# The first norm's modulation vectors in plain fp32 through four column groups of TensorE, and a new order of the first 190 steps

## The chip, the cores and the metric

One core of one Trainium2 chip runs the whole block. The metric is the device time of one launch in microseconds (us), median of several runs. The engines are named as in the profile: PE is TensorE's matmuls, PEld its weight loads, DVE VectorE, ACT ScalarE, POOL GpSimd, SP the engine whose queue issues nearly all loads.

## The reference

One layer of a diffusion block over 1024 latent tokens with 256 context tokens, width 1024, all in fp32:

```python
sh1, sc1, g1, sh2, sc2, g2 = adaln(c, w_mod, b_mod)        # silu(c) @ w_mod + b_mod, in six pieces
csh1, csc1, ... = adaln(c_ctx, w_mod, b_mod)
hc = modulate(ctx, norm1_w, csh1, csc1)                     # rmsnorm(x) * w * (1 + scale) + shift
state = context_state(hc, w_in, b_in)
h = modulate(x, norm1_w, sh1, sc1)
out, _ = token_mixers(h, w_in, b_in, ..., state, grid=True)
x = x + g1 * out
x = x + g2 * ffn(modulate(x, norm2_w, sh2, sc2), w_ff1, w_ff2)
return rmsnorm(x, final_norm_w)
```

The change concerns sh1, sc1, csh1, csc1 alone: two vectors (c and c_ctx) times the first 2048 columns of w_mod, 8 MB of weights.

## The kernel before

A large product is made from two fp32r halves of each operand, hi (the rounded value) and lo (the rest): three matmuls (hi hi, hi lo, lo hi) take the place of one in fp32. ACT rounds hi, DVE or POOL subtracts for lo.

The first stage ends with the keys, queries and first values of heads 0 and 1. It is written out by hand in ORDER: a list of steps, each a letter and a number, and every engine's instructions keep this order. Each engine's queue runs in order, so an instruction that waits holds up all behind it on its engine. The steps:

- mN loads piece N (128 x 1024, 512 KB) of the modulation weights; 2k and 2k+1 are the two halves of the contraction for feature block k (128 features; shift and scale for them).
- oN makes the lo half of piece N where it has one, on DVE or POOL (LO_G).
- rk is the matmuls of feature block k: the stationary operand is silu of the two vectors, the moving one the weights, the result a PSUM bank "o". yk copies it to SBUF (mrow). ck turns it with the small matrix comb from rows into columns (PSUM tile psu), and DVE adds the bias and forms 1 + scale (mod1).
- xN, hN, nN load a tile of 128 tokens, square and sum it on ACT, and scale it on DVE to xh. Tiles 0 to 3 are the first half of the tokens, 4 to 7 the second, 8 and 9 the context.
- fgk, ugk, jgk take feature block k of token group g (g is left out for 0): f transposes four tiles on PE, u applies the modulation and rounds to hh, j subtracts for hl. For odd k, u runs on ACT and j on POOL, else DVE.
- w, z load and split the weights of keys (w0) and queries (w1); gk is the six matmuls of 512 columns that add feature block k to keys and queries. v, b load and split the value weights (v0s), t and s make the values of a chunk of 128 tokens. e takes keys and queries out of PSUM.

Keys and queries of a token half need all eight feature blocks, so g7 waits for the last modulation piece. PSUM banks "o" exist twice, "g" three times, others once. After the list, the rest of the kernel follows: recurrence, gates, output projections and the MLP. Its code is not touched. SP's loads are issued in order, and each waits for the landing of the load eight places before it.

Before, ten of the sixteen pieces are split into hi and lo (whi, wlo, with the vectors split too, silr), six (F32N) are used in fp32 with the vectors in sil4:

```python
for j in range(4):
    for i, (a, w_) in enumerate(ops):
        PE.matmul(b, a[:, 4 * (n % 2) + j, :], w_[:, j * 256 : j * 256 + 256], ...)
```

All four j add into the same four rows of the bank, b[0:4].

Of the kernel before, what the change touches and what calls it, by code (L numbers as in the profile page):

```python
# [22 lines left out]
NPG = 37  # L23
NPG2 = 4
PUMP = 1300.0
F32N = (1, 2, 3, 4, 5, 8)
LO_G = (1, 4, 5, 6, 9, 11, 12, 15)

ORDER = (
# [6 lines left out]
)  # L36
MOD_RATE = 0.16
YC = 448
# [11 lines left out]
CST = {}  # L50
_off = 0
for _name, _n in (("ident", 128), ("mask", 256), ("ones", 128), ("ident2", 128), ("flip", 128), ("dsel", 128), ("t2", 64), ("tri", 256), ("e", 8), ("sel", 16), ("selt", 128), ("selc", 16), ("selct", 32), ("ec", 2), ("comb", 2)):
    if _name == "ident2":
        NCST0 = _off
# [6 lines left out]
def tile_block(ctx: ExitStack, tc: tile.TileContext, x, cx, w_mod1, w_mod, w_v0, w_v, w_unit, w_conv, w_mls, w_o, w_f1, w_f2, cols_d, rows_d, cst_d, out):  # L61
# [20 lines left out]
    V, A, G, PE, SY = Engine(nc.vector), Engine(nc.scalar), Engine(nc.gpsimd), Engine(nc.tensor), nc.sync  # L82

    cpool = ctx.enter_context(tc.tile_pool(name="cpool", bufs=1))
    dpool = ctx.enter_context(tc.tile_pool(name="dpool", bufs=1, space=bass.MemoryType.DRAM))
    pg = ctx.enter_context(tc.tile_pool(name="pg", bufs=NPG))
    ws = ctx.enter_context(tc.tile_pool(name="ws", bufs=2))
# [5 lines left out]
    def dma(dst, src, pin=True):  # L93
        i = SY.dma_start(dst, src)
        if pin:
            tc.keep_in_program_order(i)
# [3 lines left out]
    def nm(s):  # L100
        uid[0] += 1
        return f"{s}_{uid[0]}"

    def page(shape, dt=F32, name="pg"):
        return pg.tile(shape, dt, tag="pg", name=nm(name))

    def half(name):
        return ws.tile([P, 512], F32, tag="half", name=nm(name), bufs=4)

    cols = cpool.tile([P, NCOL], F32, name="cols")  # L110
    cst0 = cpool.tile([P, NCST0], F32, name="cst0")
# [84 lines left out]
    def bank(tag="g"):  # L196
        if tag == "g":
            pool = psg
            if psg2:
                pool = (psg, psg2[0])[turn[0] % 8 > 2]  # L200
                turn[0] += 1
            return pool.tile([P, 512], F32, tag="g", name=nm("psg"))
        return psm.tile([P, 512], F32, tag=tag, name=nm("ps" + tag), bufs=2 if tag == "o" else 1)
# [3 lines left out]
    A.activation(sig, col("c2", 0, 16), AF.Sigmoid)  # L207
    sil = cpool.tile([P, 8, 2], F32, name="sil")
    V.tensor_tensor(sil, col("c2", 0, 16).rearrange("p (v k) -> p k v", v=2), sig.rearrange("p (v k) -> p k v", v=2), op=ALU.mult)
    silr = cpool.tile([P, 8, 4], F32R, name="silr")  # L210
    V.tensor_copy(silr[:, :, 0:2], sil)
    V.tensor_tensor(silr[:, :, 2:4], sil, silr[:, :, 0:2].bitcast(F32), op=ALU.subtract)
    sil4 = cpool.tile([P, 8, 4], F32, name="sil4")
    V.memset(sil4, 0.0)
    V.tensor_copy(sil4[:, :, 0:2], sil)

    eps_c = cpool.tile([P, 1], F32, name="eps_c")
    V.memset(eps_c, EPS)
# [16 lines left out]
        dma(st, src)  # L235
        return wide(st, **kw)

    dma(cst0, cst_d[:, :NCST0])

    def rstd_of(xt, scratch):  # L240
        ss = ws.tile([P, 1], F32, tag="ss", name=nm("ss"))
        keep(A.activation)(scratch, xt, AF.Square, accum_out=ss)
# [10 lines left out]
        return b[:, : len(tiles) * P]  # L253


    comb = ws.tile([4, 2], F32, tag="comb", name="comb", bufs=1)
    dma(comb, cst_d[0:4, CST["comb"][0] : CST["comb"][0] + 2])
    mcol = bank("u")
    loads, lows = {}, {}
    mod1 = cpool.tile([P, 2, 2, 8], F32, name="mod1")  # L260
# [2 lines left out]
    def mod_load(n):  # L263
        w = page([P, 1024], name="wmod")
        dma(w, w_mod1[n // 2, n % 2])
        if n in F32N:
            return [(sil4, w)]
        hi, lo = [page([P, 1024], F32R, t_) if n % 2 else ws.tile([P, 1024], F32R, tag=t_, name=nm(t_)) for t_ in ("whi", "wlo")]
        A.activation(hi, w, AF.Copy)
        lows["o", n] = lambda: (G if n in LO_G else V).tensor_tensor(lo, w, hi.bitcast(F32), op=ALU.subtract)  # L270
        return [(silr, hi), (silr, lo)]

    def mod_rows(k):

        b = bank("o")[0:4, 0:256]
        for n in (2 * k, 2 * k + 1):
            ops = loads.pop(n)
            for j in range(4):
                for i, (a, w_) in enumerate(ops):
                    PE.matmul(b, a[:, 4 * (n % 2) + j, :], w_[:, j * 256 : j * 256 + 256], start=n % 2 == 0 and j == 0 and i == 0, stop=n % 2 == 1 and j == 3 and i == len(ops) - 1)  # L280
        return b

    def mod_cols(k, r):
# [67 lines left out]


    gb = wm.tile([P, 32], F32, name="gb", bufs=1)
    dma(gb, rows_d[0:1, 1024:1056].to_broadcast([P, 32]))

    gz = wm.tile([P, 2, 160], F32, tag="e", name="gz", bufs=3)

    def v_out(p):
        vb = wm.tile([P, 256], F32, tag="vb", name=nm("vb"), bufs=1)
        dma(vb, rows_d[0:1, p * 256 : p * 256 + 256].to_broadcast([P, 256]), pin=p == 0)  # L360
        va = [page([P, 2, 4, 129], name="va") for _ in range(2)]
        vc = wm.tile([P, 2, 2, 129], F32, tag="vc", name=nm("vc"), bufs=1)
        for t_ in (*va, vc):
            G.memset(t_[:, :, :, 128:129], 1.0)
        return va, vc, vb
# [332 lines left out]
    vs0 = (*v_out(0), wv0, 288)  # L698
# [28 lines left out]
    def item(i):  # L727

        op, n = i[0], int(i[1:])
        g, k = divmod(n, 10)
        if op == "m":
            loads[n] = mod_load(n)
        elif op in "obz":
            lows.pop((op, n), int)()
        elif op == "r":
            made[op, n] = mod_rows(n)  # L740
        elif op == "y":
            r = half("mrow")[0:4, 0:256]
            V.tensor_copy(r, made.pop(("r", n)))
            made[op, n] = r
        elif op == "c":
            mod_cols(n, made.pop(("y", n)))
        elif op == "x":
            load(n)
        elif op == "h":
            square(n)  # L750
        elif op == "n":
            hat(n)
        elif op == "f":
            if n == 20:
                for h_ in (hch, hcl):
                    h_ += [page([P, 1024], F32R, "hc") for _ in range(2)]
            made[op, n] = transposed(TILES[g], k)
        elif op == "u":
            hi, _, sh, sc = feat(g, k)
            made[op, n] = modulate(made.pop(("f", n)), hi, sh, sc, k)  # L760
        elif op == "j":
            hi, lo, _, _ = feat(g, k)
            (G if k % 2 else V).tensor_tensor(lo, made.pop(("u", n)), hi.bitcast(F32), op=ALU.subtract)
        elif op == "w":
            st = ws.tile([P, 1024], F32, tag="wst", name=nm("wst"))
            dma(st, w_unit[(U_K, U_Q)[n]])
            hi, lo = page([P, 1024], F32R, "whi"), page([P, 1024], F32R, "wlo")
            A.activation(hi, st, AF.Copy)
            lows["z", n] = lambda: V.tensor_tensor(lo, st, hi.bitcast(F32), op=ALU.subtract)
            wkq.append((hi, lo))  # L770
        elif op == "g":
            if k == 0:
                accs[g] = [bank(), bank()]
            gemm_k(wkq, hT, g, accs[g], k)
        elif op == "e":
            evac_k(0, kT0, accs[n][0], n)
# [238 lines left out]
    m2 = cpool.tile([P, 4, 8], F32, name="m2")  # L1015
# [262 lines left out]
    t2 = [None] * KT  # L1278
# [230 lines left out]
    b12, b22, t1, t4, t2_ = (lambda k: feat2(f1, k)), (lambda k: feat2(f1, 4 + k)), (lambda k: feat2(f0, k)), (lambda k: feat2(f0, 4 + k)), (lambda k: feat2(t2f, k))  # L1509
# [177 lines left out]
    for i in range(tail):  # L1687
        m, k = steps[i]
# [3 lines left out]
        o = Y if m in (5, 6, 3) else X  # L1692
# [9 lines left out]
        if i == 3:  # L1702
            g2 = grow(3, Y[0:2])
# [9 lines left out]
        if k == NP - 1:  # L1713
# [17 lines left out]
            elif m == 3:  # L1731
                a, b, c, d = [gated_sum(j, R, Y[j], ub[j]) for j in (2, 3, 0, 1)]
# [8 lines left out]
    for j in range(4):  # L1741
        t = 4 + j
        cuts = (0, 512) if j < 3 else (0, CUT, 512)
        n = len(cuts)
# [5 lines left out]
        for c in range(1, n):  # L1750
            s = slice(cuts[c - 1], cuts[c])
            w = cuts[c] - cuts[c - 1]
# [24 lines left out]
def _layout(i):  # L1777
# [11 lines left out]
    o = {}  # L1789
# [6 lines left out]
    v0 = np.concatenate([wv[:, 0:256], w_in[:, 1536:1568]], axis=1)  # L1796
# [19 lines left out]
    r = np.arange(P)  # L1816
# [10 lines left out]
    sel = (d_ * 8 + h_)[:, None] == dh[None, :]  # L1827
    selc = ((rc // 16) * 8 + rc % 8)[:, None] == dh[None, :]
    comb = np.zeros((P, 2))
    comb[[0, 2], 0] = 1  # L1830
    comb[[1, 3], 1] = 1
    cst = {
        "ident": eye, "ident2": eye, "flip": eye[::-1], "dsel": (d_[:, None] == d_[None, :]) * 1.0,
        "t2": (r[:, None] % 64 == np.arange(64)[None, :]) * 1.0,
# [28 lines left out]
```

## Time and profile before

| | |
|---|---|
| median of 3 runs | 1784.93 us (1784.78 to 1785.35) |
| profiled execution | 1784.66 us |
| its span | 1782.9 us |
| PE busy | 1738.9 us (98%) |
| DVE, ACT, POOL busy | 1269.6, 754.8, 192.8 us |
| mean DMA rate | 146 GB/s; 325 in the first fortieth of the span |
| PE, first work | at 11.21 us |

The span is the stretch from the first to the last instruction; the profiled execution's time has 1.8 us around it. Times below are counted from the span's start. An idle time in a row stands in brackets with what ended it. A matmul in fp32 shows as two records (it runs in two passes), one in fp32r as one. Records of a matmul overlap with the next, so work is read from start to start.

### The profile page before, as it was taken

The page shows a single profiled execution, that of the slowest core. Times are in us where ns is not written, and L with a number is a line of the kernel's source. Part 1 is how long each engine was busy: PE and PEld are TensorE (multiplying, and loading weights), DVE is VectorE, ACT ScalarE, POOL GpSimd, SP SyncE. Part 2 cuts the span into 40 slices and gives each one's busy share as a digit, 9 for nine tenths or more (in the row PEclk, how much of TensorE's full clock was granted, in tenths as well). Part 3 has the DMA queues.
Part 4 walks back from the last instruction along what each step waited for, and adds up shares of the span by engine and source line. Part 5 has one row for each costly group of instructions (what it writes and reads, how often), then busy time and mean ns, then how long its engine had stood idle before and what let it go on. Part 6 is the DMA issues. An engine that isn't in the chain of part 4 may idle for free.

```text
span 1782.9 us, 23518 instructions
## 1 busy us (share of the span) xinstructions
PE 1738.9 (98%) x8633; PEld 1433.6 (80%) x8633; DVE 1269.6 (71%) x2224; ACT 754.8 (42%) x1239; POOL 192.8 (11%) x269
## 2 busy tenths in 40 slices
PE   7999999999999999999999999999999999999994
PEld 3898889877878888888888888877888888888884
DVE  5557565564876669878889987877666656577785
ACT  5633544556343332222244435644444354343434
POOL 3202122212300000000000001111011000000001
PEclk9999999999999999999999999999999999999997
DMA  8213131321534452433647255135334285665352
GB/s 325 77 47 91 46 93 43 89 70 61 174 145 142 157 197 97 140 131 124 228 167 284 71 207 183 72 138 187 130 141 178 112 279 194 233 230 199 104 181 94
DMA packets 102108, 261.11 MB, mean 146 GB/s; under 512 B 11624, under 2 KB 24808, under 8 KB 101992
## 3 DMA queue, kind: packets, MB, share of 16 engines
q1 hardware_dynamic: 85672, 200.88, 34.5%
q0 software_dynamic: 16320, 58.73, 8.3%
q8 instruction: 67, 1.10, 0.3%
q14 instruction: 49, 0.40, 0.1%
HBM read 198.62 MB, written 60.95 MB: 146 GB/s over the span
## 4 chain that ended last, share of the span: by engine, by line
PE 65%; DVE 4%; ACT 2%; issue 1%; ACTq 0%; DVEq 0%
PE psg L75 65%; ACT y L75 1%; DVE wlo L75 1%; DVE gate L75 0%; DVE wst L75 0%; ACT Fsh L75 0%; DVE y L75 0%; ACT fc L75 0%; DVE fc L75 0%; DVE Gv L75 0%; DVE x L75 0%; DVE ftmp L75 0%; DVE Ff L75 0%; DVE Fsl L75 0%; DVE u L75 0%
## 5 line engine op out<-in xcount | busy, mean ns | idle before, releaser
L75 DVE TENSOR_TENSOR wlo<-wst,whi 128x512 fp32r<-128x512 f32 (+1 forms) x236 | 223.5, 950 | 144.5 <-ACT whi L75 144.0
L75 ACT ACTIVATE whi<-wst 128x512 fp32r<-128x512 f32 (+1 forms) x238 | 195.8, 826 | 262.4 <-PE psg L75 170.4
L75 PE MATMUL psg<-whi,wlo 128*128 128x512 f32 (+2 forms) x688 | 266.2, 387 | 0.0
L75 PE MATMUL psg<-whi 128*128 128x512 f32 (+2 forms) x688 | 266.2, 387 | 0.0
L75 PE MATMUL psg<-wlo,whi 128*128 128x512 f32 (+2 forms) x688 | 265.7, 386 | 0.1
L75 PE MATMUL psg<-hh,whi 128*128 128x512 f32 x440 | 176.0, 406 | 0.0
L75 PE MATMUL psg<-hh,wlo 128*128 128x512 f32 x440 | 172.7, 398 | 1.3 <-DVE wlo L75 1.3
L75 PE MATMUL psg<-hl,whi 128*128 128x512 f32 x440 | 172.0, 397 | 0.0
L75 PEld LDWEIGHTS psg<-wlo,whi 128*128 128x128 f32 x688 | 129.3, 188 | 28.0 <-DVE wlo L75 0.6
L75 PEld LDWEIGHTS psg<-whi,wlo 128*128 128x128 f32 x688 | 129.2, 188 | 27.3
L75 PEld LDWEIGHTS psg<-whi 128*128 128x128 f32 x688 | 129.2, 188 | 27.0
L75 PEld LDWEIGHTS psg<-hh,wlo 128*128 128x128 f32 x440 | 83.1, 189 | 20.5 <-DVE wlo L75 1.7
L75 PEld LDWEIGHTS psg<-hl,whi 128*128 128x128 f32 x440 | 83.1, 189 | 17.3
L75 PEld LDWEIGHTS psg<-hh,whi 128*128 128x128 f32 x440 | 82.4, 189 | 17.9
L75 PE MATMUL psg<-oh,Fsl 128*128 128x512 f32 x240 | 94.8, 395 | 0.1
L75 PE MATMUL psg<-oh,Fsh 128*128 128x512 f32 x240 | 94.9, 395 | 0.0
L75 PE MATMUL psg<-ol,Fsh 128*128 128x512 f32 x240 | 94.5, 394 | 0.0
L75 DVE TENSOR_TENSOR u<-psg,u 128x512 f32<-128x512 f32 x67 | 45.8, 686 | 51.5 <-PE psg L75 51.5
L75 PE MATMUL psg<-whi,hh 128*128 128x256 f32 (+1 forms) x256 | 76.0, 297 | 0.0
L75 PE MATMUL psg<-wlo,hh 128*128 128x256 f32 (+1 forms) x256 | 73.2, 286 | 0.0
L75 PE MATMUL psg<-whi,hl 128*128 128x256 f32 (+1 forms) x256 | 73.1, 286 | 0.0
L75 POOL TENSOR_TENSOR wqz<-w,q 64x256 f32<-64x256 f32 x64 | 48.9, 768 | 159.1 <-PE pso L75 141.2
(347 smaller groups left out, 3868.3 us busy)
## 6 DMA issues: line engine op xcount, KB each, us to landing
wst<-fq SPq DMA_DIRECT2D x112, 256.0 KB, 2.8
wst<-in_w_unit_dram SPq DMA_DIRECT2D x38, 512.0 KB, 5.2
mst<-in_w_mod_dram SPq DMA_DIRECT2D x32, 512.0 KB, 4.3
fq<-Ff POOLq DMA_DIRECT2D x32, 512.0 KB, 4.2
wst<-in_w_f_dram SPq DMA_DIRECT2D x64, 256.0 KB, 3.1
wst<-in_w_f_dram SPq DMA_DIRECT2D x21, 512.0 KB, 4.3
Hwst<-in_w_unit_dram SPq DMA_DIRECT2D x18, 512.0 KB, 5.2
x<-in_x_dram SPq DMA_DIRECT2D x16, 512.0 KB, 6.0
```

The source lines that it names most:

```text
L75: i = f(*a, **kw)
```

## The change

All sixteen pieces are used in fp32. The vectors stand in sil32, whose rows 2 to 31 are zero, so that a matmul fills 32 columns of the array; the four j of a piece go to four groups of 32 columns and to four groups of 32 rows of the bank (rows 32j and 32j+1 hold the result). comb, now 128 rows, adds the four groups up in ck. The splits of the modulation weights and steps o are gone. The loads of comb and of the first constants (cst0, with the identity for transposes) move from the front into a step k0, those of the biases gb and vb into a step l0. The list is in a new order up to where the second half begins, and beyond it.

```diff
-    silr = cpool.tile([P, 8, 4], F32R, name="silr")
...
-    V.tensor_copy(sil4[:, :, 0:2], sil)
+    sil32 = page([P, 8, 32], name="sil32")
+    G.memset(sil32, 0.0)
+    V.tensor_copy(sil32[:, :, 0:2], sil)
...
-    dma(cst0, cst_d[:, :NCST0])
...
-        if n in F32N:
-            return [(sil4, w)]
-        hi, lo = [page([P, 1024], F32R, t_) if n % 2 else ws.tile([P, 1024], F32R, tag=t_, name=nm(t_)) for t_ in ("whi", "wlo")]
-        A.activation(hi, w, AF.Copy)
-        lows["o", n] = lambda: (G if n in LO_G else V).tensor_tensor(lo, w, hi.bitcast(F32), op=ALU.subtract)
-        return [(silr, hi), (silr, lo)]
+        return w
...
-        b = bank("o")[0:4, 0:256]
+        b = bank("o")[:, 0:256]
         for n in (2 * k, 2 * k + 1):
-            ops = loads.pop(n)
+            w = loads.pop(n)
             for j in range(4):
-                for i, (a, w_) in enumerate(ops):
-                    PE.matmul(b, a[:, 4 * (n % 2) + j, :], w_[:, j * 256 : j * 256 + 256], ...)
+                PE.matmul(b[32 * j : 32 * j + 32, :], sil32[:, 4 * (n % 2) + j, :], w[:, j * 256 : j * 256 + 256], start=n % 2 == 0, stop=n % 2 == 1, skip_group_check=True)
...
-            r = half("mrow")[0:4, 0:256]
+            r = half("mrow")[:, 0:256]
...
+        elif op == "k":
+            dma(comb, cst_d[:, CST["comb"][0] : CST["comb"][0] + 2])
+            dma(cst0, cst_d[:, :NCST0])
+        elif op == "l":
+            dma(gb, rows_d[0:1, 1024:1056].to_broadcast([P, 32]))
+            dma(vs0[2], rows_d[0:1, 0:256].to_broadcast([P, 256]))
...
-    "x0 m0 x2 h0 m1 x3 o1 h3 o0 x1 n3 m2 m3 m4 h2 n2 o3 h1 r0 n1 o4 o2 y0 n0 r1 y1 c0 m6 f0 m5 m7 m9 o5 o6 f1 u0 r2 m8 y2 c1 "
+    "m3 x2 x1 x3 h3 x0 h2 h0 n2 h1 m2 m0 r1 n3 m1 n0 r0 y1 k0 n1 m7 f0 y0 f1 m4 c0 c1 f2 m5 u0 m6 r2 r3 y2 m8 j0 c2 u1 m9 "
...
```

What it does to the order, on PE at the very start. Before, the last pair of r0's first piece (split) and its second piece (in fp32, with sil4, here sil), then r1, c and the transposes of f0:

```order
L75 MATMUL pso_187<-whi_143,silr 4x256
L75 MATMUL pso_187<-wlo_144,silr 4x256
L75 MATMUL pso_187<-wmod_153,sil_86 4x256 x4
L75 MATMUL pso_208<-wmod_168,sil_86 4x256 x4
L75 MATMUL pso_208<-wmod_170,sil_86 4x256 x4
L75 MATMUL psu_95<-comb,mrow_203 128x2 x2
L75 MATMUL psm_60_228<-cst_67,xh_148 128x128
```

Now r1, r0, and then the transposes of f0:

```order
L73 MATMUL pso_169<-wmod_165,sil_2_83 32x256 x4
L73 MATMUL pso_169<-wmod_132,sil_2_83 32x256 x4
L73 MATMUL pso_186<-wmod_167,sil_2_83 32x256 x4
L73 MATMUL pso_186<-wmod_181,sil_2_83 32x256 x4
L73 MATMUL psm_55_204<-cst_67,xh_152 128x128
```

Each r is eight matmuls of 32 rows by 256 columns where it was eight to sixteen of 4 rows by 256; the first transposes come before the first use of comb.

On SP, the first loads before (x the tokens, wmod the pieces m):

```order
L94 DMA cols<-in_cols_dram 128x168
L94 DMA cst_67<-in_cst_dram 128x512
L94 DMA comb<-in_cst_dram 4x2
L94 DMA gb<-in_rows_dram 128x32
L94 DMA vb_131<-in_rows_dram 128x256
L94 DMA x_139<-in_x_dram 128x1024
L94 DMA wmod_141<-in_w_mod_dram 128x1024
L94 DMA x_146<-in_x_dram 128x1024
```

And now, from the start:

```order
L92 DMA cols<-in_cols_dram 128x168
L92 DMA wmod_132<-in_w_mod_dram 128x1024
L92 DMA x_134<-in_x_dram 128x1024
L92 DMA x_136<-in_x_dram 128x1024
L92 DMA x_138<-in_x_dram 128x1024
L92 DMA x_145<-in_x_dram 128x1024
L92 DMA wmod_165<-in_w_mod_dram 128x1024
L92 DMA wmod_167<-in_w_mod_dram 128x1024
L92 DMA wmod_181<-in_w_mod_dram 128x1024
L92 DMA comb<-in_cst_dram 128x2
L92 DMA cst_67<-in_cst_dram 128x512
```

Four small loads left the front; the four token tiles and the first pieces moved up. gb and vb now stand behind the weights of keys and queries (w0, w1), and m15 behind the first value weights.

On PE where the products g begin (hh, hl are the modulated tokens; whi and wlo the split weights of keys and queries where they stand with them, of a piece m where they stand with silr). Before, the end of r5's 16 matmuls, behind g0 and g1, and then g2:

```order
L75 MATMUL pso_413<-whi_346,silr 4x256
L75 MATMUL pso_413<-wlo_347,silr 4x256
L75 MATMUL psg_379<-hh_99,whi_282 128x512
L75 MATMUL psg_380<-hh_99,whi_333 128x512
L75 MATMUL psg_379<-hl_107,whi_282 128x512
L75 MATMUL psg_380<-hl_107,whi_333 128x512
```

Now, the end of g0, then c4, r5 and g1:

```order
L73 MATMUL psg_333<-hh_92,wlo_273 128x512
L73 MATMUL psg_334<-hh_92,wlo_299 128x512
L73 MATMUL psu_90<-comb,mrow_308 128x2 x2
L73 MATMUL pso_353<-wmod_311,sil_2_83 32x256 x4
L73 MATMUL pso_353<-wmod_306,sil_2_83 32x256 x4
L73 MATMUL psg_333<-hh_93,whi_272 128x512
L73 MATMUL psg_334<-hh_93,whi_298 128x512
```

Before, g2 was followed by r6 and r7, and g3 to g7 came behind them; now it is g0, c4, r5, g1, c5, r6, g2, c6, r7, f7, g3, c7, and g4 to g7. Behind g7 the instructions on PE are the same as before, in another order: t1, then three transposes of the second token half, t2, and so on.

## Rows read from the trace of the kernel before

**Rows 1.** Windows, whole core: length, busy (instructions) of PE, PEld, DVE, ACT, POOL; PEclk, DMA share.

```profile
11.20:59.02 47.82, 45.28 (x241) 28.00 (x241) 35.41 (x55) 30.88 (x48) 20.71 (x9) 0.96 0.71 270
59.02:107.29 48.27, 48.27 (x338) 45.95 (x336) 19.12 (x51) 24.93 (x45) 8.16 (x10) 1.00 0.13 47
107.29:1760.00 1652.71, 1645.10 (x8059) 1359.61 (x8057) 1203.58 (x2087) 684.73 (x1118) 158.45 (x237) 1.00 0.43 145
```

**Rows 2.** Groups by form, PE, 11.2 to 59.02.

```profile
L75 PE MATMUL pso<-wmod,sil 128*4 128x256 f32 x48 | 12.9, 430 | 0.0
L75 PE MATMUL pso<-whi,silr 128*4 128x256 f32 x40 | 10.4, 294 | 11.2 <-ACT whi L75 11.2
```

**Rows 3.** Timeline, PE, 11 to 36: start, us, engine, operation, count.

```profile
14.06 7.38 PE L75 MATMUL pso<-wmod,sil 128*4 128x256 f32 x24
21.36 0.60 PE L75 MATMUL psu<-comb,mrow 4*128 4x2 f32 x4
...
22.92 3.62 PE L75 MATMUL pso<-wmod,sil 128*4 128x256 f32 x16
...
33.95 0.60 PE L75 MATMUL psm<-cst,xh 128*128 128x128 f32 x4
34.39 0.60 PE L75 MATMUL pso<-cst,xh 128*128 128x128 f32 x4
```

**Rows 4.** Windows at the changes of the granted clock.

```profile
18.20:38.70 20.50, 19.23 (x117) 11.48 (x116) 15.21 (x26) 13.37 (x16) 9.78 (x5) 1.00 0.90 360
38.70:42.10 3.40, 3.40 (x9) 2.18 (x10) 3.40 (x3) 0.30 (x1) 3.40 (x2) 0.50 0.70 221
```

**Rows 5.** Timeline, PE, 39 to 59.

```profile
39.11 1.05 PE L75 MATMUL psg<-hh,whi 128*128 128x512 f32 x2
39.97 1.05 PE L75 MATMUL psg<-hl,whi 128*128 128x512 f32 x2
...
57.64 0.63 PE L75 MATMUL psg<-hh,whi 128*128 128x512 f32 x2
58.11 0.62 PE L75 MATMUL psg<-hl,whi 128*128 128x512 f32 x2
```

**Rows 6.** Timeline, PE, the instant 219.9, and what follows.

```profile
219.68 0.28 PE L75 MATMUL psg<-whi,hl 128*128 128x256 f32 x1
219.88 0.38 PE L75 MATMUL psm<-q,kT 64*128 64x128 f32 x2
...
220.31 0.39 PE L75 MATMUL psg<-whi,hh 128*128 128x256 f32 x1
```

**Rows 7.** Timeline, ACT, 10 to 29.

```profile
10.10 1.06 ACT L75 ACTIVATE whi<-wmod 128x1024 fp32r<-128x1024 f32 x1 [5.74 <-DMA wmod<-in_w_mod_dram]
...
13.96 1.06 ACT L75 ACTIVATE xh<-x 128x1024 f32<-128x1024 f32 x1 [1.44 <-DMA x<-in_x_dram]
...
24.14 1.06 ACT L75 ACTIVATE whi<-wmod 128x1024 fp32r<-128x1024 f32 x1 [0.22 <-DMA wmod<-in_w_mod_dram]
...
27.75 0.78 ACT L75 ACTIVATE mtmp<-pso,mod 128x512 f32<-128x512 f32 x1 [2.03 <-PE psm L75]
28.56 0.63 ACT L75 ACTIVATE hh<-mtmp 128x512 fp32r<-128x512 f32 x1
```

**Rows 8.** Groups by form, ACT, 11 to 59.02.

```profile
L75 ACT ACTIVATE whi<-wmod 128x1024 fp32r<-128x1024 f32 x10 | 10.3, 1049 | 9.6 <-DMA wmod<-in_w_mod_dram 9.6
```

**Rows 9.** Groups by form, DVE, 11 to 59.02.

```profile
L75 DVE TENSOR_TENSOR wlo<-wmod,whi 128x1024 fp32r<-128x1024 f32 x5 | 7.6, 1515 | 7.7 <-ACT whi L75 7.7
...
L75 DVE COPY mrow<-pso 4x256 f32<-4x256 f32 x8 | 3.3, 409 | 4.6 <-PE pso L75 4.6
```

**Rows 10.** Groups by form, POOL, 11 to 59.02.

```profile
L75 POOL TENSOR_TENSOR wlo<-wmod,whi 128x1024 fp32r<-128x1024 f32 x5 | 14.0, 2813 | 25.4 <-ACT whi L75 25.4
L75 POOL TENSOR_TENSOR hl<-mtmp,hh 128x512 fp32r<-128x512 f32 x4 | 6.8, 1697 | 9.5 <-ACT hh L75 9.5
```

**Rows 11.** DMA rate over 0 to 40, in 40 slices of 1 us.

```profile
GB/s 0 52 157 169 82 210 329 401 418 414 426 410 422 426 397 410 418 414 397 430 422 397 426 410 406 401 414 418 406 401 422 410 410 397 414 324 89 41 24 59
```

More of the change, by code (lines that the diff above doesn't have):

```diff
@@ L25 @@
 PUMP = 1300.0
-F32N = (1, 2, 3, 4, 5, 8)
-LO_G = (1, 4, 5, 6, 9, 11, 12, 15)
 ORDER = (
[6 rows of a table removed]
[6 rows of a table added]
 )
@@ L209, in tile_block @@
     V.tensor_tensor(sil, col("c2", 0, 16).rearrange("p (v k) -> p k v", v=2), sig.rearrange("p (v k) -> p k v", v=2), op=ALU.mult)
-    silr = cpool.tile([P, 8, 4], F32R, name="silr")
[L211 to L214, printed above, removed]
-    V.tensor_copy(sil4[:, :, 0:2], sil)
+    sil32 = page([P, 8, 32], name="sil32")
+    G.memset(sil32, 0.0)
+    V.tensor_copy(sil32[:, :, 0:2], sil)
     eps_c = cpool.tile([P, 1], F32, name="eps_c")
@@ L253, in transposed @@
         return b[:, : len(tiles) * P]
-    comb = ws.tile([4, 2], F32, tag="comb", name="comb", bufs=1)
-    dma(comb, cst_d[0:4, CST["comb"][0] : CST["comb"][0] + 2])
+    comb = ws.tile([P, 2], F32, tag="comb", name="comb", bufs=1)
     mcol = bank("u")
@@ L265, in mod_load @@
         dma(w, w_mod1[n // 2, n % 2])
-        if n in F32N:
-            return [(sil4, w)]
-        hi, lo = [page([P, 1024], F32R, t_) if n % 2 else ws.tile([P, 1024], F32R, tag=t_, name=nm(t_)) for t_ in ("whi", "wlo")]
-        A.activation(hi, w, AF.Copy)
-        lows["o", n] = lambda: (G if n in LO_G else V).tensor_tensor(lo, w, hi.bitcast(F32), op=ALU.subtract)
-        return [(silr, hi), (silr, lo)]
+        return w
     def mod_rows(k):
-        b = bank("o")[0:4, 0:256]
+        b = bank("o")[:, 0:256]
         for n in (2 * k, 2 * k + 1):
-            ops = loads.pop(n)
+            w = loads.pop(n)
             for j in range(4):
-                for i, (a, w_) in enumerate(ops):
-                    PE.matmul(b, a[:, 4 * (n % 2) + j, :], w_[:, j * 256 : j * 256 + 256], start=n % 2 == 0 and j == 0 and i == 0, stop=n % 2 == 1 and j == 3 and i == len(ops) - 1)
+                PE.matmul(b[32 * j : 32 * j + 32, :], sil32[:, 4 * (n % 2) + j, :], w[:, j * 256 : j * 256 + 256], start=n % 2 == 0, stop=n % 2 == 1, skip_group_check=True)
         return b
@@ L353, in tile_block @@
     gb = wm.tile([P, 32], F32, name="gb", bufs=1)
-    dma(gb, rows_d[0:1, 1024:1056].to_broadcast([P, 32]))
     gz = wm.tile([P, 2, 160], F32, tag="e", name="gz", bufs=3)
@@ L359, in v_out @@
         vb = wm.tile([P, 256], F32, tag="vb", name=nm("vb"), bufs=1)
-        dma(vb, rows_d[0:1, p * 256 : p * 256 + 256].to_broadcast([P, 256]), pin=p == 0)
+        if p:
+            dma(vb, rows_d[0:1, p * 256 : p * 256 + 256].to_broadcast([P, 256]), pin=False)
         va = [page([P, 2, 4, 129], name="va") for _ in range(2)]
@@ L736, in item @@
             loads[n] = mod_load(n)
-        elif op in "obz":
+        elif op in "bz":
             lows.pop((op, n), int)()
@@ L1829, in _layout @@
     comb = np.zeros((P, 2))
-    comb[[0, 2], 0] = 1
-    comb[[1, 3], 1] = 1
+    for v in range(2):
+        comb[v::32, v] = 1
     cst = {
```

10 rows, old and new, of the table ORDER are left out of this document.

## The prediction, made before the changed kernel ran

> **What bounds the kernel now.** I read the windows first. From 59.02 to 107.29, the second half of the hand-ordered stage, PE is busy all the time, and from there to 1760 it misses 7.6 of 1652.7 us [rows 1]. So a microsecond that PE gains before 59.02, where g7 ends, is kept if the stretch behind finds its data in time. Ahead of it lie two costs: 11.2 us in which PE waits for the first split piece [rows 2], and 47.8 us with 45.3 us of work [rows 1]. In that work the groups by form show the modulation matmuls: 12.9 us in fp32, and 10.4 us for the hi records, with as many lo records between them [rows 2]; some 24 us in all from start to start.
>
> The timeline gives prices from start to start. At full clock eight fp32 matmuls (16 records) take 3.62 us, so 0.226 a pass; a step c takes 0.54 (21.36 to the next work), a step f 0.44 [rows 3]. A step g takes three times 0.47, 1.40 us, late in the stage [rows 5]. PE begins at half clock (1.2 GHz): 24 records of the same kind that begin at 14.06 need 7.38 instead of 24 by 0.226, 5.4 [rows 3]. At 18.2, some 6 us after its matmuls began to run densely, the clock is full; it falls once more for 3.4 us from 38.7 [rows 4], where PE has just waited for a low half, and there g takes 2.6 [rows 5].
>
> The loads come next. The rate is full (about 410 GB/s) only from 7 us on, since small rows stand in front, and stays full to 35 [rows 11]. ACT starts on pieces the moment they land: the second 512 KB at 10.10, the thirteenth at 24.14 [rows 7], so 1.28 us each. PE can't use a piece before it lands, and sixteen pieces, four token tiles and w0, w1 are 28 us of loads. The stage is bound by both, and the change touches both.
>
> **The change, part by part.**
>
> *Splits removed.* ACT loses ten roundings (10.3 us), DVE five subtractions (7.6), POOL five (14.0) [rows 8, 9, 10]. None is the bound of the whole stage; it counts in that an r follows its load directly, and that PE need not stand where it stood at 11.2 and 38.
>
> *Matmuls.* Before, 24 us. Now 64 fp32 matmuls, 128 passes. One group at a time that is 128 by 0.226, 29 us: more than before. Four at a time it is 7.2. The trace of before has no column groups. The nearest row is a pair in two groups of 64 rows: at 219.88 two matmuls start together, one 0.37 long, and both passes of both are over when the next work starts 0.43 later [rows 6], two passes' time and not four. So groups do run side by side, pass by pass. It also shows the change of shape costing: 0.20 from the 256-column matmul ahead to the pair where 0.12 would do (a quarter of the 0.47 for two times 512 columns [rows 5]), and some 0.2 behind. I take four at a time plus 0.2 for the change of shape: 4 passes by 0.226, 1.1 us for one r. Bounds: 1.0 and 3.8.
>
> The Trainium skill speaks against it (TensorE: Matmul & The Clock Gate, "The mechanism"): a weight load overlaps running matmuls only where the row group differs, and four column groups share all rows. By that rule the second rival below would be likelier. The same page measures 2.38 for three column tiles, which would make r about 1.5 us and the end, an estimate, 1775.
>
> *Steps c* use 128 rows instead of 4: same passes, same 0.54. *y* copies 128 rows instead of 4, in the same columns: 0.41 as before [rows 9], or at the most 0.5, a third of what DVE takes for 128 rows of four times the columns [rows 9]. The memset of sil32 lies in the first idle 10 us.
>
> *Loads.* Four small ones leave the front. With full rate from 2.2 us (the first load lands about then) the sixth big piece, m2, lands at 10.1, m1 at 12.6, w1 at 23.5, and m15, behind 22 big pieces and 1.8 pieces of small ones, at 32.5. If full rate comes only at 7 as before, m15 lands at 35. gb and vb with their small rows now stand in mid stream, so I take a piece's delay: m15 at 33.6.
>
> *The order on PE, as a chain.* r1 starts with m2, r0 ends at 13.7 (half clock). f0 waits for the fourth normalised tile: ACT squares four tiles from 7.4, 1.06 each [rows 7] and an allowance of 0.3 for the root, and DVE scales the last, for which I allow 1.2: 14.1. From 14.1 to g0 stand six f, four c and three r: 2.6 + 2.2 + 3.3 = 8.1 us at full clock. If the clock rises at 20, as it did 6 us into dense work, that ends at 25.2. g0's low halves are DVE's work behind y4 (23.9), for which I take 1.1 each, since POOL has nothing beside them (the mean of the same shape was 1.5 [rows 9], which would make it 0.8 later): 26.1, and g0 ends at 26.7. Then c4, r5, g1, c5, r6, g2, c6: 1.6 + 2.2 + 2.8 = 6.6, 33.3. So PE and the last piece come to r7 together; r7 ends at 34.4. f7, g3, c7 and g4 to g7 are 0.44 + 0.54 + 7.0 = 8.0: 42.4. c7 ends at 36.8; its u7 stands on ACT behind the square of a token tile (to 38.8), takes 0.78 + 0.63 [rows 7], and j7 on POOL 1.7 [rows 10]: 41.9. g7 waits for it half a microsecond and ends at 43.0, not 59.0.
>
> *Behind g7* the same 48.3 us of PE work follow [rows 1]. In the old order the tiles x4 to x7 had long landed; now x5 lands at about 40, and its square queues on ACT behind the two value splits and another square, so that f15 starts near 46.5 where t1 ends at 46.2. Then ACT has keys and queries to take out of PSUM before it can free a bank for f13. I put 2 us on these waits, with 1 and 5 as ends. The stage ends at 93.3 instead of 107.3: 14.0 us. The value loads and the first gates follow in the same distance as before.
>
> *The clock.* PE now meets more waits early, so I add one more half-clock stretch than the chain has: 3.4 us at half speed, 1.7 lost (0 to 4.6, the latter with half clock up to g0). 14.0 − 1.7 = 12.3. Against the profiled execution, 1784.66: **1772.4 us**; that execution lies 0.27 under the median of 1784.93.
>
> **The rivals.**
>
> *Two at a time.* The second pass of a group holds up the first pass of the next (the row pair speaks against it, but it lies in row groups). r takes 2.0; six of them, r2 to r7, lie on the chain, 0.9 each: 5.4 less. 1777.8.
>
> *One at a time.* Groups that share rows and a bank don't overlap, and every r pays the change of shape: 3.8 us. Then r1 and r0 alone last to 20.8, and PE is the bound throughout: f0, f1, c0, c1, f2 to 23.2, r2, r3 to 30.8, c2, f4, r4, f5, f3, f6, c3 to 37.4, then g0, c4, r5, g1, c5, r6, g2 to 50.3, and c6, r7 and the 8.0 behind it to 62.6. Slower by 3.6 where nothing waits behind: 1788.3. It decides from 3.1 us an r on, where the gain is gone (12.3 over six is 2.05 above 1.1), and is slower by over 0.2% from 3.7. Rows 6 speak against it.
>
> *The second half starves.* PE is early, x4 to x7 and the value weights are not: their loads stand last in SP's queue, and those pages are free only when PE has done earlier work. If x4 is held until the g steps, about 40, the four tiles land at 45, are normalised by 50, and everything behind waits 4 to 8 us. 1779.
>
> *The change does nothing*, since the loads bound the stage anyway: the last piece was there at 35 before [rows 11] and g7 ended 24 us later, so that isn't so.
>
> **How the numbers follow.** Forecast 0.59, with 1767 to 1776 its own range (all waits small and the clock full: 43.0 less 3, as m15 at 32.5 allows; half clock to g0 and 2 us more of waits). Two at a time 0.18, one at a time 0.10, starved 0.13. The range leaves out the third rival and the tail of the fourth: 1767 to 1781. A change of 0.2% is 3.6 us, about what a measurement of this kernel can tell from none: faster 0.82 (forecast 0.58, two at a time 0.17, starved 0.07), same 0.10, slower 0.08.
>
> **What would show it.** r as a block of 16 records in 1.1 us from start to start, with four starts within a few hundredths of a microsecond; PE's first matmul near 10; m15's r7 near 34; g7's end between 41 and 48; the start of the first product behind the stage (kcT, from hc) between 91 and 98 where it was 107.3. I am wrong if r takes over 3 us, if PE stands more than 5 us in all between g7 and that point, or if the granted clock stays half beyond 30.

## The result, and the profile after

| | |
|---|---|
| changed kernel | 1772.99 us median of 4 runs (1771.89 to 1773.45) |
| before, same chip | 1784.91 us median of 4 runs (1784.78 to 1785.35) |
| ratio | 0.9933, 95% interval 0.9921 to 0.9945: 11.9 us faster |
| profiled execution | 1773.45 us, span 1771.7 us |

Windows of the changed kernel, columns as in [rows 1]: the stretch to g7's end, the one to the start of kcT, and 1652.71 us of the rest as in [rows 1]; then two stretches at half clock, beside [rows 4].

```profile
11.60:46.61 35.01, 31.65 (x240) 21.78 (x241) 21.56 (x49) 18.67 (x31) 5.94 (x4) 0.90 0.87 348
46.61:95.95 49.34, 48.61 (x338) 46.05 (x336) 18.22 (x50) 25.77 (x48) 8.29 (x10) 1.00 0.13 42
95.95:1748.66 1652.71, 1644.37 (x8059) 1359.91 (x8057) 1201.08 (x2090) 685.29 (x1119) 157.66 (x237) 1.00 0.44 145
17.70:21.10 3.40, 3.08 (x22) 1.40 (x22) 1.36 (x4) 1.90 (x3) 0.00 (x0) 0.50 1.03 417
31.40:34.80 3.40, 3.40 (x18) 2.64 (x20) 1.14 (x5) 0.01 (x1) 0.00 (x0) 0.50 1.03 419
```

These rows show that all of the gain lies ahead of 46.6: g7 ends 12.4 us earlier than before (59.02), the stretch behind it is 1.07 us longer (49.34 against 48.27), and the rest is PE work as before. Ahead of 46.6 PE has 31.65 us of work in place of 45.28, and 3.4 us of idling.

PE's timeline there, beside [rows 2, 3, 5]; the rows of `pso<-wmod,sil` are the r (the first holds r1 and r0), those of `hh,whi` begin a step g:

```profile
11.60 3.25 PE L73 MATMUL pso<-wmod,sil 128*32 128x256 f32 x32 [11.60 <-DMA wmod<-in_w_mod_dram]
...
26.09 0.72 PE L73 MATMUL psg<-hh,whi 128*128 128x512 f32 x2
...
27.59 0.50 PE L73 MATMUL psu<-comb,mrow 128*128 128x2 f32 x4
30.08 1.07 PE L73 MATMUL pso<-wmod,sil 128*32 128x256 f32 x16 [1.98 <-DMA wmod<-in_w_mod_dram]
31.08 0.98 PE L73 MATMUL psg<-hh,whi 128*128 128x512 f32 x2
...
34.34 1.27 PE L73 MATMUL pso<-wmod,sil 128*32 128x256 f32 x16
...
37.47 1.07 PE L73 MATMUL pso<-wmod,sil 128*32 128x256 f32 x16
...
46.15 0.62 PE L73 MATMUL psg<-hh,wlo 128*128 128x512 f32 x2
...
95.95 0.40 PE L73 MATMUL psg<-hc,whi 128*128 128x256 f32 x2
```

An r takes 1.00 us from start to start (30.08 to 31.08), with PE busy for 1.07; before, eight fp32 matmuls kept PE busy for 3.62 [rows 3]. In the instant behind the start of r5, four matmuls are under way:

```profile
30.08 0.42 PE L73 MATMUL pso<-wmod,sil 128*32 128x256 f32 x4 [1.98 <-DMA wmod<-in_w_mod_dram]
```

The two largest waits on PE in the first 110 us (us in total, times, longest):

```profile
PE pso L73 <- DMA wmod<-in_w_mod_dram: 13.6, 2, 11.6
PE pso L73 <- ACT mtmp L73: 0.7, 1, 0.7
```

Of the 13.6 us for pieces, 11.6 lie ahead of the first matmul and 1.98 ahead of r5 at 30.08. The rate of the loads, in slices of 1 us, beside [rows 11]:

```profile
GB/s 0 27 190 352 397 393 418 418 422 418 422 422 396 376 414 410 410 410 410 418 422 414 418 368 65 328 411 406 422 414 425 406 429 416 429 410 414 414 414 413
```

It is full from about 4 us, not from 7, and has a hole at 24 to 26. The copies y, now of 128 rows, take 0.42 us each on DVE (groups by form, 11.6 to 46.61) where they took 0.41 [rows 9]:

```profile
L73 DVE COPY mrow<-pso 128x256 f32<-128x256 f32 x8 | 3.4, 420 | 3.7 <-PE pso L73 3.7
```

### The profile page after: what moved, and what is told of

Its sections match the earlier page's. It is cut to its first block, busy times and chain, and to the rows that moved or that the text cites. A ratio compares the mean times of both kernels' runs of the same rounds, so it can differ in the third digit from the quotient of the medians.

```text
span 1771.7 us, 23486 instructions
## 1 busy us (share of the span) xinstructions
PE 1724.8 (97%) x8633; PEld 1427.8 (81%) x8633; DVE 1252.1 (71%) x2216; ACT 745.5 (42%) x1229; POOL 177.6 (10%) x265
## 4 chain that ended last, share of the span: by engine, by line
PE 67%; DVE 3%; ACT 2%; issue 1%; ACTq 0%; DVEq 0%
PE psg L73 67%; ACT y L73 1%; DVE wst L73 0%; ACT Fsh L73 0%; DVE y L73 0%; ACT fc L73 0%; DVE fc L73 0%; DVE wlo L73 0%; DVE x L73 0%; DVE ftmp L73 0%; DVE Ff L73 0%; DVE Fsl L73 0%; DVE ol L73 0%; DVE f L73 0%; ACT fd L73 0%
## 5 line engine op out<-in xcount | busy, mean ns | idle before, releaser
L73 PEld LDWEIGHTS psg<-hh,whi 128*128 128x128 f32 x440 | 82.1, 188 | 19.1 <-issue 0.8
```

The lines of the kernel that those rows point to most:

```text
L73: i = f(*a, **kw)
```

## The experiments

All twelve, with the parts of the change that each holds ("late" small loads stand where the changed kernel has them). Beside them the kernel before took medians of 1784.5 to 1784.9 us:

| kernel | order | small loads | splits | column groups | us, median (range) |
|---|---|---|---|---|---|
| before | old | front | yes | none | 1784.9 |
| e12 | old | front | dead work | 4 | 1783.7 (1780.5 to 1785.7) |
| e3 | old | front | none | 4 | 1775.6 (1773.0 to 1778.3) |
| e6: e3 and warm-up | old | front | none | 4 | 1775.7 (1774.1 to 1776.9) |
| e7 | new | front | none | 4 | 1775.4 (1774.3 to 1775.9) |
| e9 | old | late | none | 4 | 1773.05 (1772.7 to 1773.7) |
| changed kernel | new | late | none | 4 | 1773.0 (1771.9 to 1773.5) |
| e8 | new | late | none | 4, group by group | 1773.3 (1772.9 to 1773.7) |
| e2 | new | late | none | 2 | 1776.3 (1774.9 to 1776.5) |
| e1 | new | late | none | 1 | 1791.0 (1789.6 to 1791.4) |
| e10 | new | late | dead work ahead of r | 4 | 1792.0 (1791.8 to 1792.7) |
| e5: warm-up | new | late | none | 4 | 1772.0 (1771.5 to 1772.3) |
| e4 | new | gb, vb later still | none | 4 | 1771.7 (1771.5 to 1772.2) |
| e11 | new, m15 ahead of v0 | as e4 | none | 4 | 1771.2 (1770.9 to 1771.5) |

### How many groups (e1, e2, e8)

e1 puts all four j into one group, e2 into two; y and c take 32 and 64 rows.

```diff
-PE.matmul(b[32 * j : 32 * j + 32, :], ..., start=n % 2 == 0, stop=n % 2 == 1, ...)
+PE.matmul(b[0:32, :], ..., start=n % 2 == 0 and j == 0, stop=n % 2 == 1 and j == 3)       # e1
+PE.matmul(b[32 * (j % 2) : 32 * (j % 2) + 32, :], ..., start=n % 2 == 0 and j < 2, ...)   # e2
```

Expected of e1:

> The changed kernel, but all eight matmuls of an r go to one group of 32 columns (rows 0 to 31 of the bank), one after the other; y and c take 32 rows instead of 128. Order, loads and full precision stay. If the four column groups are what makes the change pay, an r takes 3.6 to 3.8 us from start to start instead of 1.03, PE is the bound from the first piece on, g7 ends near 62 us instead of 46.6, and the time is 1785 to 1788 us. If the new order and the missing splits make the gain and the groups only add to it, the loads hide most of the longer r and the time stays below 1777 us.

Expected of e2:

> The changed kernel, but the four matmuls of a piece go to two groups of 32 columns, two to each. If groups run side by side pass by pass, an r takes 1.9 to 2.0 us; r0 to r4 lie partly in the 3 us that PE idles or stands at half clock before g0, r5 in its 2 us wait for its piece, so that 2 to 4 of the 7 us added show: 1774.5 to 1777 us. If a group's second pass holds up the next group's first (two at a time, the recorded rival), four groups would have been no better than two and r stays at 1.03 us with the time at 1773.

PE's timeline of e1, r5 and the start of g1 behind it:

```profile
40.20 3.64 PE L73 MATMUL pso<-wmod,sil 128*32 128x256 f32 x16
43.77 0.72 PE L73 MATMUL psg<-hh,whi 128*128 128x512 f32 x2
```

The same two in e2:

```profile
33.00 1.92 PE L73 MATMUL pso<-wmod,sil 128*32 128x256 f32 x16
34.85 0.73 PE L73 MATMUL psg<-hh,whi 128*128 128x512 f32 x2
```

An r takes 3.57, 1.85 and 1.00 us with one, two and four groups: side by side as many as there are. e2 came out as the first theory had it (1776.3). e1 is slower than before by 0.35% (ratio 1.0035, 1.0021 to 1.0048), 3 us above what was expected: g7 ends at 63.4 and not at 62, and another 1.3 us are spread over the matmuls behind the stage, with no wait of their own. If the time rises evenly from e2 to e1, an estimate, the gain is gone at an r of about 2.8 us (1.85 + 8.2 us by 1.72/14.7).

e2's r is hardly shorter than an r of before whose two pieces are both split, such as r3. PE's timeline of the kernel before, its start and the next work (1.96 us later):

```profile
28.12 0.28 PE L75 MATMUL pso<-whi,silr 128*4 128x256 f32 x1
...
30.08 1.89 PE L75 MATMUL pso<-wmod,sil 128*4 128x256 f32 x8
```

So most of the gain, 8.2 of 11.9 us, is there with an r about as long as a split one was. Of the r, only those with unsplit pieces (3.62 us for two) are much shorter in e2; the section on the splits tells what else pays.

e8 issues the same eight matmuls group by group, so that neighbours in the queue share a group.

```diff
-for n in (2 * k, 2 * k + 1):
-    w = loads.pop(n)
-    for j in range(4):
+ws_ = {n: loads.pop(n) for n in (2 * k, 2 * k + 1)}
+for j in range(4):
+    for n, w in ws_.items():
```

Expected of e8:

> The changed kernel with the eight matmuls of an r issued group by group (both pieces of group 0, then of group 1, and so on) and not group after group. If neighbours on the queue must stand in different groups to run side by side, the 16 passes fall to 13 one after another, an r takes 2.7 to 3 us and the time is 1780 to 1785 us. If the array holds back and overlaps whatever the order, r stays near 1.03 us and the time near 1773.

PE's timeline of e8, r5 and what follows:

```profile
30.24 1.09 PE L73 MATMUL pso<-wmod,sil 128*32 128x256 f32 x16 [1.33 <-DMA wmod<-in_w_mod_dram]
31.26 0.50 PE L73 MATMUL psg<-hh,whi 128*128 128x512 f32 x1
```

The instant behind its start:

```profile
30.24 0.45 PE L73 MATMUL pso<-wmod,sil 128*32 128x256 f32 x4 [1.33 <-DMA wmod<-in_w_mod_dram]
```

The second theory held: 1.02 us, again four under way at once, 1773.3 us. The order in which an r is issued doesn't matter; over how many groups it is spread does (e1, e2).

### The splits (e12, e10)

e12 is the old order with before's splits on the same engines at the same places, but unused.

```diff
+if n not in F32N:
+    hi, lo = ...
+    A.activation(hi, w, AF.Copy)
+    lows["o", n] = lambda: (G if n in LO_G else V).tensor_tensor(lo, w, hi.bitcast(F32), op=ALU.subtract)
 return w
```

Expected of e12:

> The order of before with its steps o and its splits on the same engines at the same places, but as dead work: the r take the unsplit pieces in four column groups. Beside the old order without splits (1775.6 us) this gives the price of the splits' engine time where it stood before, which putting them ahead of each r in the new order (1792.0) doesn't. If PE's matmuls are the gain and ACT, DVE and POOL had room for the splits in that order, 1775 to 1777 us. If the engine time that came free is a part of the gain, 1779 us or more.

The time is 1783.7 us (11 runs; ratio to before 0.9992, 0.9983 to 1.0001): the groups alone give next to nothing. PE's timeline of e12 at its longest wait:

```profile
37.77 0.63 PE L75 MATMUL psg<-hh,wlo 128*128 128x512 f32 x2
43.26 1.01 PE L75 MATMUL psu<-comb,mrow 128*128 128x2 f32 x4 [4.86 <-DVE mrow L75]
```

DVE's timeline there:

```profile
36.08 3.49 DVE L75 TENSOR_TENSOR wlo<-wmod,whi 128x1024 fp32r<-128x1024 f32 x1
39.50 0.80 DVE L75 TENSOR_SCALAR mtmp<-psm,mod 128x512 f32<-128x512 f32 x1
40.22 2.64 DVE L75 TENSOR_TENSOR wlo<-wmod,whi 128x1024 fp32r<-128x1024 f32 x1
42.79 0.41 DVE L75 COPY mrow<-pso 128x256 f32<-128x256 f32 x1
...
44.78 1.22 DVE L75 TENSOR_TENSOR wlo<-wmod,whi 128x1024 fp32r<-128x1024 f32 x1
```

POOL's, one row for three subtractions:

```profile
33.20 8.59 POOL L75 TENSOR_TENSOR wlo<-wmod,whi 128x1024 fp32r<-128x1024 f32 x3 [3.42 <-ACT whi L75]
```

PE stands for 4.86 us at c5 for mrow, the copy y5. On DVE that copy stands behind two subtractions, of 3.49 and 2.64 us, where the same shape takes 1.22 once POOL is done (44.78); POOL subtracts from 33.20 to 41.79. The Trainium skill (Trainium Architecture — The Big Picture, "What this means for kernel authors") says that DVE and GpSimd share a port pair under an exclusive lock; the stretched durations here agree with that. The window of 11 to 50 us in e12, columns as in [rows 1]:

```profile
11.00:50.00 39.00, 27.13 (x212) 16.22 (x205) 30.16 (x45) 26.07 (x39) 18.58 (x8) 0.91 0.77 310
```

The same of e3:

```profile
11.00:50.00 39.00, 33.08 (x227) 22.19 (x228) 19.07 (x45) 18.20 (x33) 4.26 (x3) 1.00 0.81 318
```

DVE has 30.2 us of work with the splits and 19.1 without, ACT 26.1 and 18.2, POOL 18.6 and 4.3. (Where no clock is recorded, a row counts it as full: in e3 up to 36.4, in e12 up to 23.6.) The loads are not what e12 loses by: its last piece lands at 36.2, e3's at 36.7. Behind the wait at c5 the granted clock was half, from 40.7 to 47.5, which makes that wait dearer. Before, PE's own matmuls were long enough for the splits to fit beside them; with groups DVE is next. The price of the splits is that of the medians, 8.1 us: the two profiled executions are the fastest of e12 and the slowest of e3, and what e12's slower runs lose beyond this one's waits was not seen.

e10 puts the dead splits into the new order, just ahead of each r.

```diff
 w = loads.pop(n)
+if n not in (1, 2, 3, 4, 5, 8):
+    A.activation(dead[n % 2], w, AF.Copy)
+    (G if g_ else V).tensor_tensor(dead[2 + g_], w, dead[n % 2].bitcast(F32), op=ALU.subtract)
```

Expected of e10:

> The changed kernel with the rounding and the subtraction of the ten pieces that were split before put back as dead work, just ahead of the r that uses the piece: ACT rounds (1.05 us each), five subtractions on DVE (1.5) and five on POOL (2.8), into four buffers that nothing else reads. If the splits cost by what PE had to wait for them and PE's own doubled records, and not by the time of the other engines, nothing changes or little: 1772.5 to 1774.5 us. If the time that ACT, DVE and POOL got back is a part of the gain, 1776 us or more.

1792.0 us, 19 more than the changed kernel. The five longest sums of PE's waits, 0 to 100 us:

```profile
PE pso L73 <- DMA wmod<-in_w_mod_dram: 11.5, 1, 11.5
PE psu L73 <- DVE mrow L73: 6.2, 3, 2.5
PE pso L73 <- DVE mrow L73: 3.9, 1, 3.9
PE psm L73 <- DVE xh L73: 2.6, 1, 2.6
PE psg L73 <- DVE hl L73: 2.0, 1, 2.0
```

The first is the wait for the first piece; the other 14.7 us are all for DVE. The clock has a share too: it was half from 18.1 to 35.2, 48.9 to 55.7 and 59.1 to 62.5, 27 us in all, where the changed kernel has 6.8 us behind the first rise. The place, ahead of each r, is a bad one, and that is part of this price; e12 has the fairer one.

### Order and small loads (e3, e7, e9, e4)

e3 is the old order without its steps o, e9 the same with the small loads late, e7 the new order with them in front, e4 the new order with gb and vb behind x5.

```diff
-"x0 m0 x2 h0 m1 x3 o1 ... m2 m3 m4 ... m10 w1 z0 ...       # before
+"k0 l0 x0 m0 x2 h0 m1 x3 ... m2 m3 m4 ... m10 w1 z0 ...    # e3
+"x0 m0 x2 h0 m1 x3 ... m2 m3 k0 m4 ... m10 w1 l0 z0 ...    # e9
+"k0 l0 m3 x2 x1 ... y1 n1 ... w1 u2 ...                    # e7, from the new order
+"m3 x2 x1 ... y1 k0 n1 ... w1 u2 ... x8 x5 l0 c7 ...       # e4, from the new order
```

Expected of e3:

> The order of before (its steps o dropped, the four small loads in front as before), with the changed kernel's full-precision pieces in four column groups. If the matmuls and the missing splits make the gain and the loads set the end of the first half, the last pieces land near 36 us in either order and the time is 1773 to 1776 us. If the new order makes the gain, 1780 us or more.

Expected of e7:

> The changed kernel with the four small loads (comb, cst0, gb, vb) in front again, steps k0 and l0 standing ahead of m3. In the old order with column groups the first big piece landed at 10.1 us with them in front, in the changed kernel at 4.9. If this order of loads is a part of the gain, every big piece up to w1 lands 3 to 4.5 us later and m10 some 2 us later, and the time is 1775 to 1776.5 us. If only the sum of bytes counts, it is 1772.5 to 1773.5 us.

Expected of e9:

> The old order with column groups, its four small loads no longer in front but where the changed kernel has them (comb and cst0 behind the eighth big load, gb and vb behind w1). The new order with small loads in front took 1775.4 us, the old order with them in front 1775.6, the changed kernel 1773.0. If the place of the small loads is all that the new order gains, this is 1772.5 to 1773.7 us. If the sequence of the other steps gains too, once the loads are early, it stays at 1774.5 us or above.

Old against new order is 1775.6 against 1775.4 with the small loads in front, and 1773.05 against 1772.99 with them late. So the new sequence of the other steps is worth nothing that these runs can tell, and the place of four small loads 2.4 to 2.5 us. The start of PE's timeline in e7:

```profile
16.74 2.73 PE L73 MATMUL pso<-wmod,sil 128*32 128x256 f32 x24 [16.74 <-DMA wmod<-in_w_mod_dram]
```

And in e9:

```profile
6.56 1.08 PE L73 MATMUL pso<-wmod,sil 128*32 128x256 f32 x8 [6.56 <-DMA wmod<-in_w_mod_dram]
```

In e7 the first r waits for m2 until 16.74, 5.1 us later than in the changed kernel (11.60), and half of these 5.1 us reach the end. In e9 r0 starts at 6.56, far earlier than in the changed kernel, and gains nothing by it. By the semaphores of the loads, w0, w1 and the last piece land at 23.8, 26.3 and 35.6 in e9, at 23.6, 24.9 and 36.0 in the changed kernel, and at 28.0, 29.3 and 39.0 in e7: the times follow these, not the first matmul.

Equal in time is not equal step by step. PE's timeline of e9 at the start of kcT:

```profile
94.27 0.40 PE L73 MATMUL psg<-hc,whi 128*128 128x256 f32 x2
```

That is 1.7 us earlier than in the changed kernel (95.95). The stretch from g7's end to kcT takes 48.1 us in the old order (e3, e6, e9), and in the new one 49.3 to 50.0 wherever g7 ends ahead of 49 (49.34 in the changed kernel, 49.96 in e4). What e9 gains by this it loses again behind kcT, in code that no run touches: 1677.0 us against 1675.7, and no wait explains it.

The runs of e3 spread over 5 us. Its profiled one is the slowest, and PE's timeline shows a step f (four transposes) at 0.85 us from start to start, 33.35 to 34.20, which is 0.44 at full clock [rows 3]:

```profile
33.35 1.06 PE L73 MATMUL psm<-cst,xh 128*128 128x128 f32 x4
34.20 1.06 PE L73 MATMUL pso<-cst,xh 128*128 128x128 f32 x4
```

The granted clock there is first recorded at 36.4, and it is full from then on: the half clock lasted that long.

Expected of e4:

> The changed kernel with step l0 (the loads of gb and vb) moved behind x5, so that they no longer stand between w1 and m11 in SP's queue. There w1 landed at 24.9 and m11 only at 28.7, 2.5 us more than a piece takes. If these two small loads hold up the rest, m10 lands near 27.5, the 2 us wait of r5 goes, perhaps with the half-clock stretch behind it, and the time is 1769.5 to 1771.5 us. If the load of v0, for which SP stands until 26.1 in any case, sets the pieces behind it, r7 waits instead and the time is 1772 to 1773 us.

1771.7 us, between the two theories. The small loads are only a part of the hole. The DMA queues (packets, MB, share of 16 engines) of the changed kernel from 25 to 28.5:

```profile
q1 hardware_dynamic: 490, 1.34, 96.6%
q8 instruction: 1, 0.02, 1.7%
```

Of e4 from 24 to 27.5:

```profile
q1 hardware_dynamic: 386, 1.41, 100.6%
q8 instruction: 1, 0.02, 2.0%
```

Of e1 from 25 to 28.5:

```profile
q1 hardware_dynamic: 414, 1.38, 99.4%
```

One packet of 0.02 MB of instructions (q8) takes 1.7% of 16 engines by 3.5 us, 0.95 us on one DMA engine; 1.1 us in e4. By the semaphores of the loads m11 lands 3.8 us after w1 in the changed kernel (both causes), 2.8 in e1 (gb and vb alone, its code packet comes at 32.0), 2.3 in e4 (the code alone), where a piece takes 1.27. So gb and vb cost 1.5 us in e1 and the code 1.0 in e4, and both together 2.5 in the changed kernel. A packet of code doesn't always cost that: in e2 (at 28.4) and e3 (at 31.8) one of 1.0 us fell among the loads, and those behind it landed 1.2 to 1.3 us apart, as elsewhere. When it delays them these runs don't show.

### The clock (e5, e6)

```diff
+for _ in range(12):                                                       # ahead of ORDER's first step
+    PE.matmul(mcol[:, 256:512], sil32[:, 0:4, :]..., sil32..., start=True, stop=True)
```

Expected of e5:

> The changed kernel with twelve fp32 matmuls of 256 columns of sil32 ahead of everything on PE, into a part of the bank of c that nothing reads, so that PE runs from 3.5 us on and not from 11.6. If the stretches at half clock (to 14.3, 17.7 to 21.1 and 31.4 to 34.8 in the changed kernel's profiled execution) cost what their work would save at the full one, the time is 1770 to 1771 us. If landings alone set g0 (26.1) and r5 (30.1), only the last stretch can count, and since PE still waits before r5 the clock may fall there as before: 1772.5 to 1773.5 us.

Expected of e6:

> The old order with column groups (as before in this study, 1775.6 us and from 1773.0 to 1778.3 among its runs, the profiled one at half clock until 36.4) and the same twelve matmuls ahead. If the clock is what the old order loses, the time is 1772 to 1773.5 us in all runs. If it loses by its sequence, it stays at 1775 us or above.

e5 took 1772.0 us, a microsecond less than the changed kernel, with ranges that overlap. Windows of e5 between its first changes of the clock:

```profile
9.10:15.90 6.80, 5.23 (x45) 2.79 (x44) 3.70 (x10) 5.44 (x12) 0.00 (x0) 1.00 1.03 409
15.90:22.70 6.80, 6.24 (x35) 4.48 (x35) 2.01 (x8) 1.80 (x3) 0.00 (x0) 0.50 1.03 415
```

PE's timeline of e5, the starts of g0, r5 and r7:

```profile
27.78 0.71 PE L73 MATMUL psg<-hh,whi 128*128 128x512 f32 x2
...
30.14 1.07 PE L73 MATMUL pso<-wmod,sil 128*32 128x256 f32 x16 [0.37 <-ACT mtmp L73]
...
36.01 1.07 PE L73 MATMUL pso<-wmod,sil 128*32 128x256 f32 x16
```

The matmuls ahead bring full clock from 9.1 on, and it falls at 15.9 all the same. g0 starts 1.7 us later than in the changed kernel (27.78, 26.09), and r5 at the same time (30.14, 30.08): its last piece lands at 29.7 (29.95), and in e5 the bank, which ACT still reads (mtmp), holds r5 for another 0.37 us. So half clock ahead of r5 costs nothing here. Behind r5 it does: in the changed kernel's profiled execution r5 to r7 take 7.39 us, at half clock from 31.4 to 34.8, and in e5 5.87 at full. For the old order the warm-up did nothing (1775.7).

### A version that is faster (e11)

```diff
-... m14 u4 r5 v0 y5 g1 m15 j4 ...
+... m14 u4 m15 r5 v0 y5 g1 j4 ...    # and l0 behind x5, as e4
```

Expected of e11:

> The kernel with gb and vb behind x5 (1771.7 us, r7 starting at 34.70 as m15 lands at 34.8), and m15 loaded ahead of v0, which stood for 4.8 us in SP's queue until its buffer was free. If r7 waits for m15, it comes up to 1 us earlier: 1770.7 to 1771.3 us. If PE itself comes to r7 no earlier than 34.7, it stays at 1771.5 to 1772 us.

1771.2 us, 13.6 below before (ratio 0.9924, 0.9911 to 0.9936), the fastest here. Its trace doesn't explain the half microsecond against e4: m15 lands at 34.0, but PE comes to r7 at 34.96 and to kcT at 94.58, no earlier than in e4 (34.70, 94.25).

## Why the prediction was right, point by point

| step | predicted | measured |
|---|---|---|
| an r, four groups | 1.1 us (1.0 to 3.8) | 1.00 |
| m2 there, first matmul | 10.1 | 11.6 |
| g0 ends | 26.7 | 27.59 |
| m15 lands | 33.6 (32.5 to 35) | 36.0 |
| r7 starts | 33.3 | 37.47 |
| g7 ends | 43.0 (41 to 48) | 46.61 |
| waits behind g7 | 2 (1 to 5) | 1.07 |
| kcT starts, with 1.7 for the clock | 95.0 | 95.95 |
| time | 1772.4 | 1772.99 |

**The matmuls.** Right, and decisive: one group would have made the kernel slower (e1), as the rival of one at a time had it (3.8 us an r and 1788.3; measured 3.57 and 1791.0); two groups cost 3.3 us where the rival of two at a time had 5.4, since r0 to r5 lie partly in PE's waits. The break-even, forecast at 3.1 us, is near 2.8. The 3.62 us that the prediction calls start to start is PE's busy time; e1's r takes 3.57 from start to start, so little hangs on it. The row pair that I followed [rows 6] carried over from row groups to column groups. PEld's timeline of the changed kernel at r7:

```profile
37.47 0.16 PEld L73 LDWEIGHTS pso<-wmod,sil 128*32 128x32 f32 x8
```

Eight weight loads, those of the second passes among them, lie within 0.16 us from the start of matmuls that run 0.4 us each. The rule of the Trainium skill that I weighed against it (TensorE: Matmul & The Clock Gate, "The mechanism"), no overlap of weight loads within one row group, does not hold for these four groups, which share all rows and give 3.57 times one group's rate. The 2.38 for three tiles on the same page of the Trainium skill would have made r 1.5 us, an estimate; 1.00 was measured.

**The splits.** This is the sentence that was wrong: "None is the bound of the whole stage; it counts in that an r follows its load directly". The sum came out, because its chain was made with the new work of each engine, but the sentence puts the splits too low: with groups in place, taking their time off ACT, DVE and POOL gave 8.1 us (e12 to e3), the groups alone some 1. Neither part pays without the other: without groups and without splits it is 6.5 us slower than before (e1, in the new order). The groups are what makes unsplit pieces cheap enough for PE, and e2 has most of the gain with two of them.

**Loads.** Two terms were mis-sized. Full rate came from 3.65 us (m3 landed at 4.92, less 1.27) and not from 2.2. Behind w1 the loads lost 2.5 us by gb, vb and a code packet, where the sum had about 1.1 for gb and vb and nothing for the code. These add up to 2.8 us; m15 was 2.4 us late, outside its bounds, and r5 waited 1.98 us for m10. That wait is most of the 3.6 us by which g7 was late; 0.9 lie ahead of g0's end, 1.3 are half clock behind r5, for which the sum had its 1.7 of clock allowance, and 0.6 went, since g7 did not have to wait for j7. The clock did not go as in the chain either: it was full from 14.3 and not from 20, and fell twice, from 17.7 to 21.1 and from 31.4 to 34.8. So two of the signs that the prediction named did not come: the first matmul near 10, and r7 near 34.

**Behind g7** the second half waits 1.07 and not 2 us; x4 to x7 land at 37.3 to 43.3 and come in time: the rival of a starved second half did not take place. These waits are the new order's own; the old one has none there (48.14 us in e9 against 48.27 before).

**The order.** The prediction gave the new order no term of its own beside the loads and the waits behind g7, and by e9 the whole order beside the loads is worth nothing in time. That 1772.4 came so near 1773.0 is partly luck, since errors of opposite sign met: 3.6 us late at g7, of which 1.7 was allowed for, and 0.9 gained behind.

## What to carry to other kernels

Where a matmul has few stationary columns, put independent pieces into different column groups of the array, each with its own 32 rows of the bank: four fp32 matmuls then cost about one. Before counting the gain, look at which engine is next: here the same engines' splits would have eaten nearly all of it, and only the two edits together paid. In this stage, which streams its weights, the place of small loads in the queue was worth more than the sequence of the compute steps.

## What the runs showed of the hardware that wasn't expected

- A matmul of one group starts beside those of other groups whatever the issue order: 1.02 us group by group against 1.00 (e8).
- A packet of 16 KB of instructions held one DMA engine for 0.94 to 1.09 us (changed kernel, e4). In e4 the loads behind it landed 1.0 us later, in e2 and e3 they did not. The Trainium skill (Runtime: NRT & Kernel Launch, "Instruction fetch mechanics") has these 16 KB blocks and that they come by a DMA queue; the delay to other loads is what the trace of e4 adds.
- DVE's subtraction of 128x1024 took 1.22 us alone and up to 3.49 beside POOL's (e12).
- Between kernels with the same instructions behind the stage, that stretch moved by up to 2.5 us with no new wait: from the start of kcT on it took 1674.5 us in e12, 1675.6 before, 1677.0 in e1 and in e9. A difference of one or two microseconds between two profiled executions says little of its cause.
